# The first rows of a decoder trunk, each transfer split by partitions over two issuing engines

## The chip, the cores and the metric

The kernel runs on one NeuronCore of one Trainium2 chip. The engines are named as the profile names them: PE (TensorE; PEld is its weight load), ACT (ScalarE), DVE (VectorE), POOL (GpSimd) and SP (SyncE, which issues transfers and computes nothing). The metric is the device time of one execution in microseconds (us), as the median of several runs. A profile is one more execution, taken with the hardware profiler; it has a time of its own, and a span from the first to the last instruction.

## The reference

The reference is a two-layer decoder trunk over 256 tokens of width 1024, all in float32. Layer 0 has a gated short convolution as its mixer, layer 1 an attention over shared keys and values. Each layer has a half-step feed-forward block before and after its mixer. The change touches only the start of the first block, which computes this:

```
def rmsnorm(x, g):
    y = x * lax.rsqrt(jnp.mean(x * x, axis=-1, keepdims=True) + EPS)
    return y * g

def swiglu_ffn(x, w_in, w_out):
    gate, up = jnp.split(x @ w_in, 2, axis=-1)
    return (jax.nn.silu(gate) * up) @ w_out

h = h + 0.5 * swiglu_ffn(rmsnorm(h, ffn1_norm[0]), ffn1_w_in[0], ffn1_w_out[0])
```

D_MODEL is 1024, D_FF 2816. Everything after it (mixers, attention, the other three feed-forward blocks) is the same in both kernels.

## The kernel before

**Layout.** The activations stay in SBUF, transposed: `h[c]` for c from 0 to 7 holds 128 features (partitions) by 256 tokens. A matmul is done in split precision: every operand is a high part (rounded to the fp32r type) and a low part (the rest). The high weights meet high and low activations in one matmul of 512 columns, the low weights meet the high activations in a second one of 256 columns. So every weight is first cast by ACT to its high part (`wh`) and subtracted by DVE for its low part (`wl`), and every activation likewise: ACT writes the high half of `xs` (line 293), DVE the low half (line 297).

**Weight stream.** All weights come from HBM through a class `Stream`: 1 MB pieces into one of three staging buffers `ws`, issued by SP at line 131, then cast by line 166 and subtracted by line 189. SP holds back a piece until its staging buffer is free.

**The first rows.** To start PE early, the first weight tiles (`f` 0 and 1, gate and up) do not go through the stream. On the host they are laid out between the rows of the input: the array `first` has, for each of the 128 partitions, 84 columns of gains and convolution taps, and then for every feature tile k a block of 768 columns, 256 of `x` and 512 of weights. It lands in the tile `base`. The list `cut` (line 242) divides it into seven column ranges, each a transfer over all 128 partitions, issued by SP in a loop (lines 243 and 244):

| transfer | columns | bytes in a row | KB | what it completes |
|---|---|---|---|---|
| 1 | gains, k = 0: x and weights of f = 0 | 2384 | 298 | group (0) for f = 0 |
| 2 | k = 0: weights of f = 1 | 1024 | 128 | group (0) |
| 3 | k = 1 | 3072 | 384 | group (1) |
| 4 | k = 2 | 3072 | 384 | group (2) |
| 5 | k = 3 | 3072 | 384 | group (3) |
| 6 | k = 4, 5 | 6144 | 768 | group (4,5) |
| 7 | k = 6, 7 | 6144 | 768 | group (6,7) |

After them SP issues the first two halves of a weight piece (line 252) and two more pieces (line 131).

**ACT at the start.** Its first instruction, line 247, is an activation on a single column that makes ACT load its function table while nothing else is to be done. Then it waits for the first transfer.

**PE at the start.** Eight fp32 matmuls on a tile of ones (line 257, two passes each in the trace) run while the first transfer is under way. Their results are not used.

**The work on the first rows** is `first_tiles` (lines 486 to 520). For every group of `GROUPS` it goes: high and low parts of `xs` (ACT line 293, DVE line 297), high and low parts of the weights for both f (ACT line 496, DVE line 497), after groups (1) and (3) the squares of two tiles for the norm (ACT line 484), and then PE's matmuls, high weights at line 505 and low weights at line 508, eight in all for a group of one tile. The sum of squares and its square root come later, in `first_rms`, because the scale can be applied after the matmul.

**What sets the order.** The kernel is scheduled by hand: each engine runs its instructions in the order of the program text. The framework adds the semaphores. A transfer counts a completion semaphore up as it lands; instructions that read the data wait for it. An instruction that waits holds back all that stands behind it on its engine; that holds for transfers which an engine issues, too.

Of the kernel before, what the change touches and what calls it, by code (L numbers as in the profile page):

```python
# [16 lines left out]
P = 128  # L17
# [43 lines left out]
def trunk(ctx, tc, A, out):  # L61
    nc = tc.nc
    ve, ac, pe, po, sy = nc.vector, nc.scalar, nc.tensor, nc.gpsimd, nc.sync
# [13 lines left out]
    def one(shape, name, dt=F32):  # L77
        return cp.tile(list(shape), dt, tag=name, name=name)
# [159 lines left out]
    base = one([P, G_N + ND * KW], "base")  # L238
# [2 lines left out]
    h = [kt8[:, c, :T] for c in range(ND)]  # L241
    cut = [G_N + KW - 2 * P, G_N + KW] + [G_N + (g[-1] + 1) * KW for g in GROUPS[1:]]
    for lo, hi in zip([0] + cut, cut):
        sy.dma_start(base[:, lo:hi], A["first"][:, lo:hi])
    epst = one([P, 1], "epst")
    po.memset(epst, EPS)
    ac.activation(mk([P, 1], "warm", 1), epst, AF.Sqrt)
# [1024 lines left out]
```

## Time and profile before

| | us |
|---|---|
| median of 3 runs | 975.01 (974.86 to 975.71) |
| the profiled execution | 975.94 |
| its span, first to last instruction | 974.0 |
| PE busy | 967.4 (99%) |
| DVE busy | 735.3 (75%) |
| ACT busy | 560.6 (58%) |
| POOL busy | 163.7 (17%) |

The profile page gives busy times of the engines, and a chain of work that ended last, followed back from the last instruction. Its other views are used below: the order in time of a stretch (each row a start, a duration, an engine, a source line, what is written and read, and in brackets the idle time of the engine before it and what ended it), who waited for whom, groups of instructions by line, and busy times by window. Lines are those of the kernel text above. The trace's clock starts with the span. The two microseconds between the span and the execution's time lie outside what the profile shows.

The granted clock of PE is 1.000 as a mean over the span.

### The profile page before, as it was taken

How to read it: one execution, taken by the hardware profiler on the slowest of the kernel's cores; microseconds unless marked ns; L12 is line 12 of the kernel's file. 1: busy time of each engine (PE TensorE's matmuls, PEld its weight loads, DVE VectorE, ACT ScalarE, POOL GpSimd, SP SyncE). 2: the span in 40 equal slices, each digit the busy share in tenths (PEclk: the TensorE clock that was granted, in tenths of full speed). 3: DMA queues.
4: the chain of work that ended last, by engine and by line, in shares of the span. 5: the costliest groups of instructions: out<-in, count | busy, mean ns of one | idle time of the engine just before them, and what ended most of it. 6: DMA issues, size and time to landing. Idle time of an engine off the chain costs nothing.

```text
span 974.0 us, 14801 instructions
## 1 busy us (share of the span) xinstructions
PE 967.4 (99%) x5728; PEld 848.3 (87%) x5728; DVE 735.3 (75%) x1167; ACT 560.6 (58%) x940; POOL 163.7 (17%) x256
## 2 busy tenths in 40 slices
PE   8999999999999999999999999999999999999998
PEld 7888888888888888888888888888987888888888
DVE  6988776668889887767649987965688888877752
ACT  7666553355556665644556667644488666656530
POOL 0000001144470100011211013001257240000000
PEclk9999999999999999999999999999999999999999
DMA  8665564546546875555535566554520445555550
GB/s 303 217 196 193 179 211 173 183 169 210 184 139 226 261 240 174 191 199 184 205 130 174 180 223 208 210 182 176 212 88 2 135 168 193 196 179 201 189 189 22
DMA packets 28290, 177.61 MB, mean 182 GB/s; under 512 B 3083, under 2 KB 6539, under 8 KB 7612
## 3 DMA queue, kind: packets, MB, share of 16 engines
q1 hardware_dynamic: 28220, 176.66, 53.4%
q8 instruction: 45, 0.74, 0.3%
q14 instruction: 25, 0.20, 0.1%
HBM read 175.57 MB, written 1.08 MB: 181 GB/s over the span
## 4 chain that ended last, share of the span: by engine, by line
PE 98%; DMA 1%; DVE 0%; SPq 0%; ACT 0%; issue 0%; DVEq 0%
PE mm L346 36%; PE mm L349 19%; PE a L455 17%; PE a L457 9%; PE a L346 3%; PE a L349 1%; PE mm L1012 1%; PE a L645 1%; PE a L647 1%; PE a L646 1%; DMA base<-in_first_dram 1%; PE a L1077 1%; PE a L1057 1%; PE a L933 1%; PE mm L528 1%; PE a L935 1%
## 5 line engine op out<-in xcount | busy, mean ns | idle before, releaser
L189 DVE TENSOR_TENSOR wl<-ws,wh 128x1024 fp32r<-128x1024 f32 x317 | 390.2, 1246 | 93.2 <-PE a L457 63.6
L346 PE MATMUL mm<-xs,wh 128*128 128x512 f32 x1480 | 355.8, 391 | 0.0
L166 ACT CAST wh<-ws 128x1024 fp32r<-128x1024 f32 x317 | 327.6, 1046 | 39.4 <-PE a L455 21.8
L346 PEld LDWEIGHTS mm<-xs,wh 128*128 128x128 f32 x1480 | 271.4, 188 | 52.2
L349 PEld LDWEIGHTS mm<-xs,wl 128*128 128x128 f32 x1480 | 191.0, 191 | 8.0
L349 PE MATMUL mm<-xs,wl 128*128 128x256 f32 x1480 | 193.6, 283 | 0.0
L455 PE MATMUL a<-act,wh 128*128 128x512 f32 x722 | 171.1, 390 | 0.0
L455 PEld LDWEIGHTS a<-act,wh 128*128 128x128 f32 x722 | 133.3, 188 | 26.4
L359 DVE TENSOR_TENSOR t<-mm,t 128x512 f32<-128x512 f32 x96 | 66.0, 688 | 68.7 <-ACT t L358 68.1
L358 ACT COPY t<-mm 128x512 f32<-128x512 f32 x96 | 56.1, 585 | 89.8 <-PE mm L349 88.2
L457 PEld LDWEIGHTS a<-act,wl 128*128 128x128 f32 x722 | 91.7, 191 | 2.8
L457 PE MATMUL a<-act,wl 128*128 128x256 f32 x722 | 92.9, 283 | 0.0
L293 ACT ACTIVATE xs<-base 128x256 fp32r<-128x256 f32 x48 | 24.1, 507 | 91.8 <-DVE base L422 77.6
L375 ACT ACTIVATE t<-t 128x256 f32<-128x256 f32 x88 | 36.8, 419 | 64.7 <-DVE t L363 64.7
L363 DVE TENSOR_TENSOR t<-t,R 128x512 f32<-128x512 f32 x88 | 61.6, 700 | 2.6
L352 ACT CAST act<-t 128x256 fp32r<-128x256 f32 x96 | 39.0, 407 | 29.1 <-DVE t L576 18.3
L311 POOL TENSOR_TENSOR t<-base 128x256 f32<-128x256 f32 x35 | 26.3, 751 | 135.4 <-DVE base L422 109.6
L353 DVE TENSOR_TENSOR act<-t,act 128x256 fp32r<-128x256 f32 x96 | 40.9, 426 | 5.7 <-ACT act L352 5.7
L308 POOL TENSOR_TENSOR sq<-base 128x256 f32<-128x256 f32 x5 | 3.1, 615 | 246.9 <-DVE base L422 235.4
L297 DVE SCALAR_TENSOR_TENSOR xs<-base,xs 128x256 fp32r<-128x256 f32 x48 | 29.1, 610 | 18.4 <-ACT xs L293 18.4
L376 DVE TENSOR_TENSOR t<-t,t 128x256 f32<-128x256 f32 x88 | 36.9, 420 | 4.3 <-ACT t L375 4.3
L422 DVE SCALAR_TENSOR_TENSOR base<-a,base 128x256 f32<-128x256 f32 x78 | 32.8, 421 | 7.7 <-PE a L457 6.3
(253 smaller groups left out, 866.3 us busy)
## 6 DMA issues: line engine op xcount, KB each, us to landing
ws<-in_ffn_w_in_dram SPq DMA_DIRECT2D x85, 1024.0 KB, 4.9
ws<-in_ffn_w_out_dram SPq DMA_DIRECT2D x44, 1024.0 KB, 4.8
ws<-in_conv_w_in_dram SPq DMA_DIRECT2D x12, 1024.0 KB, 4.8
ws<-in_w_kv_dram SPq DMA_DIRECT2D x6, 1024.0 KB, 4.8
ws<-in_conv_w_out_dram SPq DMA_DIRECT2D x4, 1024.0 KB, 4.8
ws<-in_attn_w_q_dram SPq DMA_DIRECT2D x4, 1024.0 KB, 4.9
ws<-in_attn_w_o_dram SPq DMA_DIRECT2D x4, 1024.0 KB, 4.9
base<-row_d SPq DMA_DIRECT2D x8, 256.0 KB, 6.4
```

The lines of the kernel that those rows point to most:

```text
L166: ac.copy(h, src)
L189: ve.tensor_tensor(out=l, in0=src, in1=h.bitcast(F32), op=ALU.subtract)
L346: pe.matmul(o, u[0][:, k * P:(k + 1) * P], xs[k], start=(k == 0), stop=False)
L349: pe.matmul(o[:, :T], u[1][:, k * P:(k + 1) * P], xs[k][:, :T], start=False, stop=(k == last))
L352: ac.copy(dst[:, :T], src)
L353: ve.tensor_tensor(out=dst[:, T:], in0=src, in1=dst[:, :T].bitcast(F32), op=ALU.subtract)
L358: ac.copy(r, o[:, :, T:])
L359: ve.tensor_tensor(out=r, in0=o[:, :, :T], in1=r, op=ALU.add)
L363: ve.tensor_tensor(out=r, in0=r, in1=R[:, None, :].to_broadcast([P, n, T]), op=ALU.mult)
L376: ve.tensor_tensor(out=s, in0=s, in1=r[:, 1], op=ALU.mult)
L455: pe.matmul(o, run[k][0], lhs[k], start=(k == 0), stop=False)
L457: pe.matmul(o[:, :T], run[k][1], lhs[k][:, :T], start=False, stop=(k == n - 1))
```

## The change

The loop body that issues one transfer of 128 partitions becomes a loop over two issuing engines. SP (`sy`) issues partitions 0 to 63 of the range, ACT (`ac`) partitions 64 to 127. The loop runs in the same place and over the same seven ranges. In ACT's order the seven new issues stand ahead of line 247.

```diff
     cut = [G_N + KW - 2 * P, G_N + KW] + [G_N + (g[-1] + 1) * KW for g in GROUPS[1:]]
     for lo, hi in zip([0] + cut, cut):
-        sy.dma_start(base[:, lo:hi], A["first"][:, lo:hi])
+        for eng, rows in ((sy, slice(0, P // 2)), (ac, slice(P // 2, P))):
+            eng.dma_start(base[rows, lo:hi], A["first"][rows, lo:hi])
```

The bytes, the rows and their lengths are the same; there are fourteen transfers in place of seven.

## Prediction

> **What bounds the kernel now.** I read the chain of work that ended last first, then the order in time of the first 14 us, because every line of the change is spent before 4 us. The page says of the whole span:
>
> ```profile
> span 974.0 us, 14801 instructions
> ...
> PE 98%; DMA 1%; DVE 0%; SPq 0%; ACT 0%; issue 0%; DVEq 0%
> ```
>
> TensorE (PE) carries the chain nearly from end to end; the change can only matter through the 1% that is DMA. The chain of the first 40 us shows where that is (start us, us, what):
>
> ```profile
> 3.06 8.45 DMA base<-in_first_dram
> 11.51 0.02 issue
> 11.54 0.91 ACT xs L293 x2
> 12.45 0.52 ACT wh L496
> ...
> 13.01 1.20 PE mm L505 x4
> ```
>
> The sixth first transfer lands at 11.51, ScalarE (ACT) prepares it, and from 13.01 on PE runs with hardly a hole. So the end of the program moves by what the matmul of 13.01 moves by, plus any slower matmuls behind it. The order in time before that point (start us, us, engine, line, idle before it in brackets):
>
> ```profile
> 0.73 1.28 ACT L247 ACT_TABLE_LOAD   x1 [0.73 <-PEq L1261]
> 0.74 3.23 SPq L244 DMA_DIRECT2D base<-in_first_dram  x7
> 1.05 3.45 PE L257 MATMUL a<-ones 128*128 128x128 f32 x16 [1.05 <-DVE ones L237]
> 2.03 0.20 ACT L247 ACTIVATE warm<-epst 128x1 f32<-128x1 f32 x1
> 3.84 0.51 ACT L293 ACTIVATE xs<-base 128x256 fp32r<-128x256 f32 x1 [1.61 <-DMA base<-in_first_dram]
> 4.01 1.92 SPq L252 DMA_DIRECT2D ws<-in_ffn_w_in_dram  x2
> 5.01 0.70 PE L505 MATMUL mm<-xs,wh 128*128 128x512 f32 x2 [0.51 <-ACT wh L496]
> 5.97 1.49 SPq L131 DMA_DIRECT2D ws<-in_ffn_w_in_dram  x2
> 6.08 0.51 ACT L293 ACTIVATE xs<-base 128x256 fp32r<-128x256 f32 x1 [1.13 <-DMA base<-in_first_dram]
> 7.25 0.70 PE L505 MATMUL mm<-xs,wh 128*128 128x512 f32 x2 [0.61 <-ACT wh L496]
> 8.70 0.51 ACT L293 ACTIVATE xs<-base 128x256 fp32r<-128x256 f32 x1 [0.88 <-DMA base<-in_first_dram]
> 9.71 0.51 ACT L293 ACTIVATE xs<-base 128x256 fp32r<-128x256 f32 x1
> 9.87 0.70 PE L505 MATMUL mm<-xs,wh 128*128 128x512 f32 x2 [0.98 <-ACT wh L496]
> 10.41 0.40 PE L508 MATMUL mm<-xs,wl 128*128 128x256 f32 x2
> 10.73 0.72 ACT L484 ACTIVATE t<-base 128x256 f32<-128x256 f32 x2
> 11.81 0.40 PE L508 MATMUL mm<-xs,wl 128*128 128x256 f32 x2
> ```
>
> Two things are to be seen. ACT waits for a landing three times, 1.61, 1.13 and 0.88 us, so it has slack early. But from 8.70 it runs through to 11.45 (10.73 + 0.72), 0.09 before its next start: whatever pushes ACT by more than that slack pushes PE. PE itself has holes of 0.61 and 0.98 us that lateness would fill first.
>
> **What a split transfer costs.** Seven issues on SyncE (SP) become fourteen, seven on SP and seven on ACT. The price of one issue by its rows (min/median/max ns), for 128 rows and for the 32 rows of a small table:
>
> ```profile
> L244 SPq DMA_DIRECT2D base<-in_first_dram x7: 388/432/432, 0.7 to 3.5; - x7
> ...
> L271 SPq DMA_DIRECT2D rb<-in_rel_bias_dram x1: 341/341/341, 263.9 to 263.9; - x1
> ```
>
> A quarter of the rows costs 341 ns against 432, so I take an issue to be a fixed cost: halving the rows saves at most 0.1 us each. SP's seven stay at 3.23 us in all (0.47 with the gap); nothing is won there. The bytes, their order and their engines' work stay too: 2 x 64 rows of the same length. The stream is already at the engines' limit before the waiting begins:
>
> ```profile
> 3.00:4.00 1.00, 1.00 (x7) 1.00 (x7) 0.00 (x0) 0.16 (x1) 0.10 (x1) 1.00 0.95 262
> ...
> 12.00:13.00 1.00, 0.91 (x6) 0.62 (x5) 0.90 (x3) 1.00 (x4) 0.00 (x0) 1.00 1.04 401
> ```
>
> The last two columns are the DMA engines' busy share and GB/s: busy 0.95 with 262 GB/s where rows are short, 401 where they are 6 KB. I keep the landings where they are: 3.84, 6.08, 8.70, 11.51. No row shows two queues feeding at once; a better overlap could bring the stream towards 401 GB/s, a worse one or unequal shares could delay it; I keep 0.8 us either way for the landing of the third transfer. [...]
>
> **What is new is on ACT.** Its seven issues stand ahead of the table load and of everything that ACT prepares, and behind them PE waits. No row shows ACT issuing; the nearest are SP's, from 0.34 us up to 0.96 (two of L252 in 1.92, the longest of the trace's start). I take 0.47 with the gap, the row of these very transfers; the ends are worth -0.1 and +0.5 where it counts, at the last issue. At this pace seven would take 0.74 + 3.23 = 4.0, and the table load and the warm activation of L247 (1.28 and 0.20) would end at 5.5. That alone costs nothing: the first rival.
>
> But an issue also has to wait. SP's waits in the first 20 us (total, times, longest):
>
> ```profile
> SPq L131 <- DMA ws<-in_ffn_w_in_dram: 7.2, 1, 7.2
> SPq L131 <- DMA base<-in_first_dram: 1.2, 1, 1.2
> ```
>
> The transfers that SP issues are seven of L244, two of L252, two of L131 (until 5.97 + 1.49 = 7.46), and the next, the twelfth, first waits 1.2 us for a *first* transfer, until 8.7. It does not read those rows; what lands at 8.7 is the fourth first transfer (ACT's start at 8.70 waits for it). Twelve minus four is eight: a transfer takes over the completion counter of the one eight places before it and waits until that has landed. I assume that both queues draw from one rotation, in program order; the trace, with one queue, cannot show it.
>
> With fourteen halves numbered SP 1, ACT 1, SP 2, ACT 2 and so on, halves 1 to 4 of each queue are free, and halves 5, 6 and 7 wait for halves 1, 2 and 3 of the same queue. ACT then goes: four issues, 0.74 to 2.6; the fifth waits for the first landing, 3.84, issue to 4.3; the sixth follows, to 4.8 (2 landed by then); the seventh waits for the third pair, 6.08, and is issued at 6.51; table load to 7.8, warm to 8.0, and the first xs of L293 starts at about 8.05 instead of 3.84: 4.2 us later. The rows that would cover a late ACT are the waits of 1.13 and 0.88 us; 4.2 is more than their sum.
>
> From there ACT has no wait left. Group 2 and 3 took 11.45 - 8.70 = 2.75 (2.66 up to where the next activation could overlap), groups 0 and 1 the same kind of work, so 5.3 in all: the xs of group (4,5) starts at 13.4 instead of 11.54, **+1.85**. PE's side: first matmul at 5.01 + 4.2 = 9.2, four groups at 1.40 (10.41 to 11.81), next at 14.85 instead of 13.01, **+1.85** as well. SP's later loads do not matter: each waits for a half eight places ahead, the fourth and fifth pairs first, and these land before 11.51, while the engines still have the sixth and seventh to move.
>
> **The clock.** PE's warm-up ends at 1.05 + 3.45 = 4.50; the next matmul now comes at 9.2, a hole of 4.7 us instead of 0.51. What a hole does is seen at both ends of the trace: the warm-up's matmuls before 3.7 and after 4.1, and the windows after the last matmul (970.9), where the column before the last two is the granted clock:
>
> ```profile
> L257 PE MATMUL a<-ones 128*128 128x128 f32 x12 | 2.9, 434 | 1.1 <-DVE ones L237 1.1
> ...
> L257 PE MATMUL a<-ones 128*128 128x128 f32 x4 | 0.7, 309 | 0.0
> ...
> 970.90:973.30 2.40, 0.00 (x0) 0.00 (x0) 0.42 (x1) 0.00 (x0) 0.00 (x0) 1.00 0.16 55
> 973.40:974.00 0.60, 0.00 (x0) 0.00 (x0) 0.00 (x0) 0.00 (x0) 0.00 (x0) 0.50 0.00 0
> ```
>
> After 2.4 to 2.5 us without a matmul the clock is halved, and at the start some 3 us of matmuls (1.05 to about 4) were needed until they ran at full speed. So a hole of 4.7 probably halves the clock, and 1 to 5 us of matmuls then run at half speed: a loss of 0.5 to 2.5, of which I take 1.4. The lower end, nothing, stays in the range. [...]
>
> **Sum.** Against the profiled execution (975.94 us, of it 974.0 span): +1.85 for ACT's late start, +1.4 for the clock, 0 for SP and the bytes: +3.2. The median of the runs is 975.01, 0.93 below that execution, so I forecast **978.2 us**. A hidden 0.1 us from added semaphore waits on ACT is within the bounds.
>
> **Rivals.**
> - *ACT is not held* (20%): the second queue has counters of its own, or waits that never bite. ACT's first xs is at 5.5; groups 0 and 1 take until 5.5 + 2.7 = 8.2, still ahead of the landing of 8.70. Late start swallowed, time 975.0, give or take 0.4. It decides at one point: whether ACT's seventh issue comes before or after 6 us. Against it: SP's wait of 1.2; for it: no trace of a second queue.
> - *Held, but the clock stays* (20%): +1.85, so 976.9, between 976.1 if the third pair lands 0.8 earlier and 977.7 if later. For it: a hole of 4.7 is not much over what was seen; the switch can fall badly or well.
> - *Two queues feed better* (4%): the landing of 11.51 comes up to 1.5 us earlier since 262 GB/s become 400, and ACT is not held; PE's holes of 0.61 and 0.98 go: 973.5. Against it: engines busy at 0.95 already, and ACT's 0.09 us of slack before 11.54.
> - *Issues of both queues exclude each other*: then eight issues end at 4.4 instead of 2.6 and ACT's seventh at about 7.2: +0.65 on the forecast, 978.9; it is inside the forecast's range.
>
> **How the numbers follow.** Forecast (held, clock halved) 56%, own range 976.9 to 980.5: 975.01 + 1.85 + 0.5 - 0.5 at the low end, with 2.5 for the clock and 0.8 for a later third landing, +0.3 for waits, at the high end. The other three cases reach down to 973.5; 974.7 to 980.5 leaves out the 4%, the lowest part of the first rival and what lies above 980.5. A measurement here tells about 0.2%, 1.95 us, from no change. Slower by more: nearly all of the forecast, 0.55, and 0.4 of the held-without-clock case, 0.08: 0.63. Faster by more would need 973.06 or less: 0.03. The rest, 0.34, is the same.
>
> **What would show it.** In the changed trace, by step: ACT's DMA issues last until after 6 us, the seventh starting as the third pair lands; the table load of L247 starts near 6.5 and the first xs of L293 near 8; PE's hole before L505 is some 4.7 us; PE's matmuls of L505 after it are longer than 0.4 us, and the granted clock shows 0.5 in a stretch between 7 and 14; the matmul that stood at 13.01 stands near 16. Wrong it would be if the table load starts before 5 (ACT not held), if the first landing or the third moves by over 1 us (two queues do change the stream), or if after the late start the clock stays at 1.0.

## The result, and the profile after

The changed kernel is slower. Six runs of each, on one chip, gave 980.12 us (979.76 to 982.09) with the change and 975.62 (974.86 to 976.12) without; the ratio of the times is 1.0052, with a 95% interval of 1.0039 to 1.0065. The profiled execution took 979.88 us against 975.94 before. Two of the six runs, 981.67 and 982.09, had a mean granted clock of 0.997 and 0.999; the other four lie between 979.76 and 980.31.

The page of the changed kernel says of the whole span (3.9 us longer) and of the chain that ended last:

```profile
span 977.9 us, 14817 instructions
...
PE 98%; DMA 0%; DVE 0%; ACT 0%; ACTq 0%; issue 0%; DVEq 0%
```

PE still carries nearly the whole chain, so the loss has to be looked for where the chain starts. The chain of the first 40 us (start us, us, what):

```profile
1.95 4.72 DMA base<-in_first_dram
...
6.70 0.47 ACTq L245
...
7.20 1.28 ACT L248
...
8.61 0.49 ACT xs L294
9.10 0.61 ACT wh L497 x2
...
9.76 1.19 PE mm L506 x2
```

Before, this chain went from the sixth landing through `xs` to a matmul at 13.01. Now it goes through ACT's own issues: a half of the third transfer lands at 6.67 (1.95 + 4.72), only then, at 6.70, does ACT make its seventh issue, and behind it come the function table, `xs`, `wh` and PE's first real matmul. The order in time of the same stretch (start us, us, engine, line, idle before it in brackets; lines are one further down than before):

```profile
0.73 6.44 ACTq L245 DMA_DIRECT2D base<-in_first_dram  x7
0.74 6.71 SPq L245 DMA_DIRECT2D base<-in_first_dram  x7
...
7.20 1.28 ACT L248 ACT_TABLE_LOAD   x1 [7.20 <-DMA base<-in_first_dram]
...
9.76 1.19 PE L506 MATMUL mm<-xs,wh 128*128 128x512 f32 x2 [4.92 <-ACT wh L497]
...
16.41 0.91 ACT L294 ACTIVATE xs<-base 128x256 fp32r<-128x256 f32 x2 [0.60 <-DMA base<-in_first_dram]
...
16.78 1.08 PE L506 MATMUL mm<-xs,wh 128*128 128x512 f32 x4
```

The table load starts at 7.20 instead of 0.73, the first real matmul at 9.76 instead of 5.01, and the matmul of group (4,5) at 16.78 instead of 13.01: 3.77 us later, nearly the 3.9 by which the span grew. Line 528, the first matmul on the weights behind `first`, moved by 3.66 (18.88 to 22.54).

SyncE waited too. Its waits in the first 30 us (total, times, longest) show three at the issues of these transfers themselves, which need no data that lands:

```profile
SPq L245 <- DMA base<-in_first_dram: 2.5, 3, 1.3
```

PE's matmuls between 9.7 and 12.4, and then between 12.8 and 16.7, by groups (count, busy us and mean ns of one, idle before):

```profile
L506 PE MATMUL mm<-xs,wh 128*128 128x512 f32 x4 | 2.2, 663 | 4.9 <-ACT wh L497 4.9
L509 PE MATMUL mm<-xs,wl 128*128 128x256 f32 x4 | 1.3, 415 | 0.0
...
L506 PE MATMUL mm<-xs,wh 128*128 128x512 f32 x12 | 3.9, 406 | 0.0
L509 PE MATMUL mm<-xs,wl 128*128 128x256 f32 x12 | 2.4, 278 | 0.0
```

The first 2.6 us of real matmuls ran at a slow clock (663 and 415 ns against 406 and 278). The granted-clock column shows 1.00 there all the same, as it does over the slow warm-up before 3.7 us in the kernel before (434 ns a matmul there, 309 after 4.1): at the start of these two traces the durations tell the clock, not that column.

What the forecast had left alone moved as well. The windows from 6 to 14 us, first of the kernel before, then of the changed one (last two columns: busy share of the DMA engines, GB/s):

```profile
6.00:14.00 8.00, 6.30 (x32) 5.03 (x31) 5.28 (x13) 6.95 (x19) 0.00 (x0) 1.00 1.01 387
```

```profile
6.00:14.00 8.00, 4.24 (x17) 3.72 (x18) 4.44 (x12) 6.79 (x19) 0.00 (x0) 1.00 1.03 260
```

The engines are as busy as before and move a third less. And the issues themselves, min/median/max in ns:

```profile
L245 ACTq DMA_DIRECT2D base<-in_first_dram x7: 472/554/618, 0.7 to 6.7; - x7
L245 SPq DMA_DIRECT2D base<-in_first_dram x7: 465/573/827, 0.7 to 7.0; - x7
```

A transfer of 64 rows costs more to issue (554 and 573 ns, median) than one of 128 did (432). "Rows" are here the partitions of a transfer, each with one row of bytes.

### The profile page after: what moved, and what is told of

The parts are those of the page before. It is cut to its first block, busy times and chain, and to the rows that moved or that the text cites. A ratio compares the mean times of both kernels' runs of the same rounds, so it can differ in the third digit from the quotient of the medians.

```text
span 977.9 us, 14817 instructions
## 1 busy us (share of the span) xinstructions
PE 968.3 (99%) x5728; PEld 849.5 (87%) x5728; DVE 735.1 (75%) x1167; ACT 560.0 (57%) x940; POOL 165.9 (17%) x256
## 3 DMA queue, kind: packets, MB, share of 16 engines
HBM read 175.57 MB, written 1.08 MB: 181 GB/s over the span
## 4 chain that ended last, share of the span: by engine, by line
PE 98%; DMA 0%; DVE 0%; ACT 0%; ACTq 0%; issue 0%; DVEq 0%
PE mm L347 36%; PE mm L350 19%; PE a L456 17%; PE a L458 9%; PE a L347 3%; PE a L350 1%; PE mm L1013 1%; PE a L646 1%; PE a L648 1%; PE a L647 1%; PE mm L506 1%; PE a L1078 1%; PE a L1058 1%; PE a L934 1%; PE mm L529 1%; PE a L935 1%
```

## The experiments

Two theories could each explain 4 us. **The hold**: ACT's issues wait for completion counters, ACT prepares nothing meanwhile, and PE starts late and at a slow clock. **The halves**: transfers of 64 neighbouring partitions move and issue more slowly, whoever issues them. The runs take them apart. The table has them all; the fifth column is by how much the first matmul of line 528 (529 to 531 elsewhere) starts later than the 18.88 of before, the last how much longer the span of the profiled execution is than 974.0. "Before" is the kernel before on the same chip.

| run | median us | before us | ratio (95%) | line 528 later | span longer |
|---|---|---|---|---|---|
| the change | 980.12 | 975.62 | 1.0052 (1.0039 to 1.0065) | 3.66 | 3.9 |
| e1_split4 | 976.50 | 975.27 | 1.0011 (1.0002 to 1.0020) | 0.17 | 0.3 |
| e2_split5 | 977.62 | 975.27 | 1.0022 (1.0012 to 1.0031) | 1.92 | 2.0 |
| e3_split6 | 978.84 | 975.27 | 1.0037 (1.0024 to 1.0050) | 3.54 | 3.6 |
| e4_sp14 | 980.56 | 975.27 | 1.0054 (1.0041 to 1.0066) | 4.26 | 4.6 |
| e5_sp14even | 986.53 | 975.46 | 1.0117 (1.0102 to 1.0132) | 10.32 | 10.6 |
| e6_evenodd | 984.62 | 975.46 | 1.0096 (1.0082 to 1.0110) | 8.23 | 8.5 |
| e7_warm26 | 979.39 | 975.46 | 1.0040 (1.0027 to 1.0052) | 3.29 | 3.6 |
| e8_holdalone | 980.37 | 975.46 | 1.0049 (1.0037 to 1.0062) | 4.48 | 4.4 |
| e9_colsplit | 980.38 | 975.33 | 1.0054 (1.0040 to 1.0068) | 3.52 | 3.5 |
| e10_sp14col | 975.98 | 975.33 | 1.0008 (0.9999 to 1.0017) | -0.48 | -0.4 |
| e11_tablefirst | 982.64 | 975.33 | 1.0077 (1.0064 to 1.0090) | 7.62 | 7.9 |
| e12_colwarm26 | 977.84 | 975.29 | 1.0026 (1.0016 to 1.0036) | 1.38 | 1.5 |

The last two columns agree within 0.4 us in every row: what the start loses arrives at the end, and nothing behind line 528 gives it back or adds to it. The medians rise by somewhat more than the spans (the change 4.5 against 3.9, e9 5.05 against 3.5): the profiled execution of the kernel before was 0.3 to 0.7 above its own medians, and those of the change, e9 and e12 were 0.24, 0.87 and 0.41 below theirs.

### Splitting only the first transfers

Three runs split the first 4, 5 or 6 of the seven transfers and leave the rest whole, on SyncE.

```diff
-    for lo, hi in zip([0] + cut, cut):
-        for eng, rows in ((sy, slice(0, P // 2)), (ac, slice(P // 2, P))):
+    for n, (lo, hi) in enumerate(zip([0] + cut, cut)):
+        halves = ((sy, slice(0, P // 2)), (ac, slice(P // 2, P))) if n < 4 else ((sy, slice(0, P)),)
+        for eng, rows in halves:
```

(5 and 6 in place of 4 for the other two.) Expected of the first:

> Only the first four of the seven transfers are split; the last three are whole, from SP. Theory H (hold): the eight halves use eight completion counters, ACT waits for none; its four issues end near 3.2 us as in the changed kernel's trace, table load to 4.5, first xs at 4.8, first real matmul at 5.95, and the landing of 8.70 swallows it: 975.6 us, within 0.5 of the kernel before. Theory S (stream): two queues of halves are slower in themselves, the loss of 4.5 us goes with the number of split transfers: 4 of 7, about +2.6, 978.2.

of the second:

> The first five transfers are split. H: ACT's fifth issue waits for its first half (3.66 in the changed trace), ends at 4.13, table load to 5.4, first xs at 5.7, first real matmul at 6.85; groups 0 and 1 are done on ACT at 8.4, before the landing near 8.7: 975.6 to 976.3. S: 5 of 7 of 4.5, about +3.2, 978.8.

of the third:

> The first six transfers are split. H: ACT's sixth issue at 5.0 as in the changed trace, ends 5.5, table load to 6.75, first xs at 6.9, first real matmul at 8.05. ACT then ends groups 0 to 3 at 12.2 instead of 11.5: +0.65, and PE's hole of 3.2 us adds 0 to 1.5 for the clock: 976.2 to 977.8. S: 6 of 7 of 4.5, about +3.9, 979.5.

The order in time of the run with four:

```profile
0.73 2.49 ACTq L246 DMA_DIRECT2D base<-in_first_dram  x4
...
3.26 1.28 ACT L249 ACT_TABLE_LOAD   x1 [3.26 <-issue]
...
13.19 1.20 PE L507 MATMUL mm<-xs,wh 128*128 128x512 f32 x4
```

With five and with six (the table load and the first real matmul of each):

```profile
4.20 1.28 ACT L249 ACT_TABLE_LOAD   x1 [4.20 <-DMA base<-in_first_dram]
...
6.76 1.19 PE L507 MATMUL mm<-xs,wh 128*128 128x512 f32 x2 [1.92 <-ACT wh L498]
```

```profile
6.40 1.28 ACT L249 ACT_TABLE_LOAD   x1 [6.40 <-DMA base<-in_first_dram]
...
8.96 1.19 PE L507 MATMUL mm<-xs,wh 128*128 128x512 f32 x2 [4.12 <-ACT wh L498]
```

Four issues wait for nothing (the table load is released by "issue"), the fifth and the sixth for a landing. The steps from 3.26 to 4.20 to 6.40 and 7.20 fit a rotation over eight counters shared by both engines, in which the fourth pair of halves is the last that finds them free. With four, the late start is swallowed up to 0.17 us at line 528; the median of its runs is still 1.23 us above the kernel before, of which its profile, 0.3 longer in the span, shows only a part. That is outside the 0.5 that the hold's theory allowed, and far below the 978.2 of the other. With five and six the loss is more than the hold's own expectation, and less than the other's. What was added is for the most part the clock: the first four groups took 8.27 us with five (6.76 to the first matmul of group (4,5) at 15.03) and 7.69 with six (8.96 to 16.65), where 5.65 is enough at full speed (below, under the clock). With five, PE's hole of only 1.92 us was followed by some 5 us of slow matmuls (two of line 507 took 1.05 us up to 12.0, 0.63 from 12.9 on); at full speed the four groups would have been done by 12.41 (6.76 + 5.65), before the 13.01 of the kernel before.

### The halves without the hold

All fourteen halves are issued by SyncE, so ACT has nothing to issue:

```diff
-        for eng, rows in ((sy, slice(0, P // 2)), (ac, slice(P // 2, P))):
+        for eng, rows in ((sy, slice(0, P // 2)), (sy, slice(P // 2, P))):
```

> All fourteen halves are issued by SP; ACT issues nothing. H: ACT's table load stands at 0.73 as before and nothing holds it; SP's issues stretch over 14 places with the waits of the rotation, the third pair is issued at 3.1 instead of 1.65: landings up to 0.7 us later, 975.6 to 976.6. If halving the transfers itself were the cost (any queue), the time would be near that of the changed kernel, 980.

Measured: 980.56, as slow as the change. The theory of the hold as the only cause fell with this run. Its order in time, issues and windows:

```profile
14.31 0.91 ACT L294 ACTIVATE xs<-base 128x256 fp32r<-128x256 f32 x2 [1.83 <-DMA base<-in_first_dram]
...
17.77 0.91 ACT L294 ACTIVATE xs<-base 128x256 fp32r<-128x256 f32 x2 [1.52 <-DMA base<-in_first_dram]
```

```profile
L245 SPq DMA_DIRECT2D base<-in_first_dram x14: 576/595/597, 0.7 to 9.0; - x14
```

```profile
6.00:14.00 8.00, 6.08 (x32) 4.70 (x30) 3.55 (x10) 4.51 (x13) 0.00 (x0) 1.00 1.04 239
```

ACT is free, and waits for landings instead: the sixth pair is there at 14.31 (11.51 before), the seventh at 17.77. Fourteen issues of 595 ns take until 9.6, and the stream moves 239 GB/s between 6 and 14 us with the engines fully busy. The last pair lands some 8 us after its issue, so here the moving sets the end more than the issuing does. This run has no loss to the clock: its first two matmuls of line 506 take 0.70 us, as before, not 1.19.

Is it the number of transfers or which partitions they cover? The next run keeps fourteen halves by SyncE and cuts by columns, so that each half covers all 128 partitions with rows half as long:

```diff
+        mid = (lo + hi) // 2
+        for eng, x0, x1 in ((sy, lo, mid), (sy, mid, hi)):
+            eng.dma_start(base[:, x0:x1], A["first"][:, x0:x1])
```

> The same column halves, all fourteen issued by SP; ACT issues nothing. P: neither hold nor slow stream is left, only fourteen issues of 0.43 to 0.6 us in a row and the waits of the rotation: third pair landed near 6.5, group (4,5) prepared near 11.6 to 12.3, time 975.5 to 976.5 (980.56 with halves by partitions). If fourteen issues from one queue cost it by themselves: 980.5 again.

Measured 975.98, 0.65 above the kernel before, with an interval (0.9999 to 1.0017) that still holds no change. Issues, windows and order in time:

```profile
L246 SPq DMA_DIRECT2D base<-in_first_dram x14: 387/432/590, 0.7 to 6.9; - x14
```

```profile
6.00:14.00 8.00, 6.52 (x35) 5.11 (x34) 5.97 (x14) 7.10 (x19) 0.00 (x0) 1.00 0.98 344
```

```profile
12.53 1.20 PE L507 MATMUL mm<-xs,wh 128*128 128x512 f32 x4 [0.93 <-DVE xs L299]
```

So fourteen transfers by themselves cost little or nothing. It is the halves of 64 partitions that issue slowly (595 against 432 ns) and move slowly (239 against 344 GB/s). Two more runs ask whether it matters that these 64 are neighbours: even partitions in one half, odd ones in the other, first all by SyncE, then shared as in the change.

```diff
+        for eng, rows in ((sy, slice(0, P, 2)), (sy, slice(1, P, 2))):
```

```diff
+        for eng, rows in ((sy, slice(0, P, 2)), (ac, slice(1, P, 2))):
```

> As the run with all fourteen halves on SP (980.56 us), but the halves are the even and the odd partitions instead of the upper and the lower 64. Theory P (port span): 64 neighbouring partitions are written at about 250 GB/s, and partitions spread over all 128 are not; a row of 6144 B takes 234 ns again (452 in the other run), group (4,5) is prepared near 12 instead of 14.3, and the time is 975.8 to 977. Theory N (any transfer of 64 rows moves at half the rate): 980.5 again.

> The change with even partitions on SP and odd ones on ACT. Under P the stream runs near 400 GB/s once rows are long, and only ACT's hold is left: seventh ACT issue near 6.3, table load near 6.8, first xs at 8.2, first real matmul at 9.4; with the clock's loss 978.3 to 979.8, little below the changed kernel's 980.1. If the slower stream were what the changed kernel pays, the time would come back to 976 to 977.

Both times missed, 986.53 and 984.62, for a reason beside the question. ACT's first cast waited for transfers that come much later, as the order in time of the first of the two shows (in the second it waited until 13.60):

```profile
15.41 0.71 ACT L497 CAST wh<-base 128x256 fp32r<-128x256 f32 x2 [10.87 <-DMA base<-in_first_dram]
```

It looks as if every second partition counted as the whole range of partitions and columns when the framework decides who waits for whom; the trace shows the wait, not the reason. The traces still answer the question. The issues are as slow as those of neighbours, here for even and odd halves by SyncE:

```profile
L245 SPq DMA_DIRECT2D base<-in_first_dram x14: 573/595/598, 0.7 to 9.0; - x14
```

So the price of an issue goes with the 64 partitions, neighbours or not; why 64 cost more than 128 no run shows. For the moving, take ACT's queue, which carries nothing but `first`. The rows give packets, MB, and the time of the packets as a share of 16 engines; of the shared even and odd halves between 9 and 12 us, of the change between 10 and 15, and of the only queue of the kernel before between 9 and 13:

```profile
q10 hardware_dynamic: 146, 0.71, 57.1%
```

```profile
q10 hardware_dynamic: 85, 0.41, 33.3%
```

```profile
q1 hardware_dynamic: 362, 1.63, 101.3%
```

57.1% of 16 engines for 3 us is 27.4 engine-us for 0.71 MB, 38.6 us for one MB; 33.3% of 16 for 5 us is 26.6 for 0.41 MB, 65 us. The kernel before needed 40 (101.3% of 16 for 4 us, 1.63 MB). So from two queues halves of every second partition move at the rate of whole transfers (38.6 against 40), and halves of 64 neighbours take 1.7 times as long for a byte. From SyncE alone, first even and odd halves between 11 and 15 us, then neighbours between 11 and 17:

```profile
q1 hardware_dynamic: 289, 1.31, 94.2%
```

```profile
q1 hardware_dynamic: 282, 1.30, 100.3%
```

That is 46 us for one MB (94.2% of 16 for 4 us, 1.31 MB, of which up to 0.4 can be weight pieces that follow `first` on this queue) against 74 (100.3% of 16 for 6 us, 1.30 MB): again the neighbours take 1.6 times as long, but here the even and odd halves don't quite reach the 40 of whole transfers. In both comparisons the halves have 64 partitions and rows of the same length; only which partitions go together differs.

The upper and lower halves from two queues, in flight together, did not make up for each other: 260 GB/s between 6 and 14 us, where whole transfers from one queue moved 387. That 64 neighbours take longer is measured; why, no run shows, and "port span" in the expectation above is only the author's name for a theory.

### The hold without the halves

The first of two runs leaves the transfers of the kernel before whole and holds ACT with copies that nothing uses, the first of which waits for the third transfer:

```diff
     ac.activation(mk([P, 1], "warm", 1), epst, AF.Sqrt)
+    held = one([P, T], "held", mybir.dt.bfloat16)
+    for _ in range(6):
+        ac.copy(held, h[1])
```

> The kernel before (seven whole transfers from SP) with six copies of 256 columns on ACT after its table load, the first of which waits for the third transfer: ACT is held until about 8.6, and nothing of the stream is changed. If the hold makes the loss: first real matmul near 9.7, 979.3 to 980.3 with the clock's loss. If the stream of halves makes it: 975 to 976.5.

The second shares halves by columns between SyncE and ACT: the change with full-width transfers.

```diff
+        mid = (lo + hi) // 2
+        for eng, x0, x1 in ((sy, lo, mid), (ac, mid, hi)):
+            eng.dma_start(base[:, x0:x1], A["first"][:, x0:x1])
```

> The change with each transfer halved by columns instead of partitions: both halves have all 128 partitions and rows of half the length; SP issues the left half, ACT the right, the same fourteen issues. Theory P (64 neighbouring partitions are slow): rows of 3072 B take some 121 ns, the stream of the long transfers runs at 330 to 400 GB/s instead of 250, the seventh pair lands near 13.5 to 14.5 instead of 16.3. Theory H (ACT's hold sets the changed kernel's end, the stream hides behind it): first xs still at 8.2 to 8.6, time 979 to 980.3. If the stream is what the changed kernel pays: 976 to 977.5.

Measured: 980.37 and 980.38, each just over the upper end of what was expected. The order in time of the first, then of the second:

```profile
6.57 2.58 ACT L250 CAST held<-base 128x256 bf16<-128x256 f32 x6 [4.34 <-DMA base<-in_first_dram]
...
10.23 1.19 PE L508 MATMUL mm<-xs,wh 128*128 128x512 f32 x2 [5.39 <-ACT wh L499]
```

```profile
6.64 1.28 ACT L249 ACT_TABLE_LOAD   x1 [6.64 <-DMA base<-in_first_dram]
...
9.20 1.19 PE L507 MATMUL mm<-xs,wh 128*128 128x512 f32 x2 [4.37 <-ACT wh L498]
```

The hold by itself makes a loss of this size too, though the copies held ACT a little longer than the change does: PE's first real matmul comes at 10.23, in the change at 9.76. The second run also gives the forecast's numbers nearly to the digit: table load at 6.64 (forecast 6.5), first matmul at 9.20 (9.2). With full-width transfers the hold is as long as I worked out; the 0.56 us more in the change (7.20, 9.76) come from the halves.

### The clock

More matmuls on ones, 26 in place of 8 (two passes each), bridge PE's hole; first in the change, then with halves by columns.

```diff
-NWARM = 8
+NWARM = 26
```

> The changed kernel with 26 warm-up matmuls instead of 8, so that PE is busy until about 8.5 us. If the clock takes 1.4 us of the loss: PE at full speed from its first real matmul near 9.8, time 978.4, range 977.9 to 979, and no executions near 982. If the clock costs nothing: 980.1.

> The column halves on SP and ACT (980.38) with 26 warm-up matmuls instead of 8. In the changed kernel these brought group (4,5) 1.4 us forward, and 1.1 of it was lost again to the late landing of the seventh pair. Column halves land earlier: if that reading is right, nothing is given back, the first matmul after the first tiles (line 528 of the kernel before) starts near 20.9 instead of 22.4, and the time is 978.6 to 979.2. If the give-back had another reason: 979.6 to 980.2.

Measured: 979.39, 0.4 above the range expected if the clock takes 1.4 us, and 977.84, below what was expected. The first order in time is that of the change with a longer warm-up, the second that of the halves by columns with it:

```profile
9.69 0.70 PE L506 MATMUL mm<-xs,wh 128*128 128x512 f32 x2 [0.16 <-ACT wh L497]
...
15.34 1.12 PE L506 MATMUL mm<-xs,wh 128*128 128x512 f32 x4
...
16.79 0.91 ACT L294 ACTIVATE xs<-base 128x256 fp32r<-128x256 f32 x2 [1.04 <-DMA base<-in_first_dram]
...
22.17 2.11 PE L529 MATMUL mm<-xs,wh 128*128 128x512 f32 x8 [0.85 <-DVE t L360]
```

```profile
8.84 0.70 PE L507 MATMUL mm<-xs,wh 128*128 128x512 f32 x2 [0.35 <-ACT wh L498]
...
20.26 2.11 PE L530 MATMUL mm<-xs,wh 128*128 128x512 f32 x8
```

The first four groups now take 15.34 - 9.69 = 5.65 us instead of 16.78 - 9.76 = 7.02: the clock cost the change 1.37. In the change most of it is given back: line 529 is only 0.37 earlier (22.54 to 22.17), because ACT waits 1.04 for the seventh pair and PE then 0.85. With full-width halves that pair is there in time and the whole gain stays: 22.40 to 20.26, 2.14, and 2.54 in the medians. That is 0.8 us below the lower end of what I expected: the four groups took 7.42 us in the run without the longer warm-up (9.20 to 16.62) and 5.66 with it (8.84 to 14.50), so 1.76 went to the clock there, and 0.36 came from a hold that ended earlier in this execution (table load at 6.28 instead of 6.64). What remains against the kernel before, 1.38 at line 528 and 2.55 in the medians, is the hold with the clock taken care of; the change with the same warm-up keeps 3.29 and 3.93, so with the clock out of the way the halves show as a cost beside the hold.

### The table load ahead of the issues

The lines of `epst` and `warm` move above the loop, so that ACT loads its table first:

```diff
+    epst = one([P, 1], "epst")
+    po.memset(epst, EPS)
+    ac.activation(mk([P, 1], "warm", 1), epst, AF.Sqrt)
     for lo, hi in zip([0] + cut, cut):
         for eng, rows in ((sy, slice(0, P // 2)), (ac, slice(P // 2, P))):
             eng.dma_start(base[rows, lo:hi], A["first"][rows, lo:hi])
-    epst = one([P, 1], "epst")
-    po.memset(epst, EPS)
-    ac.activation(mk([P, 1], "warm", 1), epst, AF.Sqrt)
```

> The changed kernel with ACT's table load and warm activation moved ahead of its seven issues. If ACT issues transfers while its table load runs: ACT's seventh issue again near 6.7, first xs at 7.2, 1.4 earlier, and the next to be late is the stream: group (6,7) waits for the landing near 16.3, its first matmul at 17.8 instead of 15.92: +1.9 to 2.4, 977.3 to 977.9. If hold alone counts and the stream costs nothing: 976.6 to 977.2 with the clock. If the table load stops ACT's issuing until 2.0: all landings 1.3 later, 980 or more.

Measured 982.64, a miss by 5 us. The order in time:

```profile
0.73 1.28 ACT L245 ACT_TABLE_LOAD   x1 [0.73 <-PEq L1262]
0.87 1.36 ACTq L248 DMA_DIRECT2D base<-in_first_dram  x2
2.26 6.25 ACTq L248 DMA_DIRECT2D base<-in_first_dram  x5
...
17.62 0.91 ACT L294 ACTIVATE xs<-base 128x256 fp32r<-128x256 f32 x2 [1.66 <-DMA base<-in_first_dram]
```

The load does not keep ACT from issuing (0.87 lies inside it), but its last issue still ended at 8.51, later than in the change (7.17), and `xs` started at 8.55 all the same. SyncE's seven ended earlier, at 6.35 (7.45 in the change), as if the counters had been dealt in another order. Behind that the last pairs came late, and ACT waited 1.92 us for one and 1.66 for another. PE stood idle for 2.06 us over the second wait, and the first four matmuls behind it took 1.65 us instead of 1.08. The time is one that the expectation gave to a table load that stops the issues, but that is not what happened. The saved table load of 1.3 us was eaten by waits, and the run tells nothing about the hold that the others don't.

## Why the prediction was right in kind and too small

**The place and the direction** were right. ACT's seven issues stand ahead of its table load; the transfers share counters that ACT has to wait for; ACT is held, PE starts late and at a slow clock. The rival in which ACT is not held would show a table load before 5 us; it starts at 7.20. The run with four splits shows where it turns: with four issues ACT is free, and 0.17 us are left of the loss at line 528.

**The counters.** The prediction had ACT's seventh issue wait for the third pair, by counting SyncE's twelfth transfer back by eight. The chain shows it: landing at 6.67, issue at 6.70. That both queues draw from one rotation was assumed; the series of four, five, six and seven splits fits it, and the run with the table load first, where ACT's issues ended later than in the change (8.51 against 7.17) and SyncE's earlier (6.35 against 7.45), suggests that the order of the rotation isn't simply the program's.

**The step that failed** is the one on the transfers: "The bytes, their order and their engines' work stay too: 2 x 64 rows of the same length", and from it "I keep the landings where they are: 3.84, 6.08, 8.70, 11.51". The bytes stayed, the engines' work did not: 65 us of engine time for one MB in place of 40. The third pair landed at 6.67 instead of 6.08, within the 0.8 that I had left open, and the last ones later still: ACT waited for the seventh until 16.41. With it fell "halving the rows saves at most 0.1 us each": halving the rows to 64 added 0.12 to 0.16 us to an issue (554 and 573 ns in the change, 595 with SyncE alone, neighbours or not, against 432). "SP's seven stay at 3.23 us in all" fell too: they took 6.71, waits for the counters among them. The row of 32 rows with 341 ns, from which I had taken a fixed cost, was of another tensor with other rows; it did not carry that far.

**The term that was mis-sized** is the hold: +1.85 at group (4,5) was forecast. Measured there are 3.77, less 1.37 for the clock: 2.4. The difference of 0.55 is that by which the table load was late (7.20 against 6.5, partly the issue itself) and the first matmul with it (9.76 against 9.2). The run with full-width halves, where the first matmul comes at 9.20, puts it on the halves: with four groups at full speed behind it, 9.20 + 5.66 = 14.86, it gives the forecast's +1.85 again. (In the forecast's own second working, 9.2 and four groups at 1.40 make 14.8, not 14.85; nothing hangs on it.)

**The clock** was forecast at 1.4 and cost 1.37. That they agree so well is luck: the 1.4 was picked from an estimated range of 0.5 to 2.5, and the same loss was 1.76 with halves by columns. And how it came about was not as described: "a hole of 4.7 probably halves the clock" supposes a clock that was up. In the changed kernel's profile all 16 warm-up matmuls were slow, as their group says (count, busy us, mean ns):

```profile
L258 PE MATMUL a<-ones 128*128 128x128 f32 x16 | 3.8, 431 | 1.1 <-DVE ones L237 1.1
```

So in this execution the hole did not halve the clock: the slow clock of the start was still there behind it. That the hole kept it from rising is my reading; the longer warm-up in the change, which has no hole and rises (427 ns a matmul between 1 and 6 us, 279 between 6.2 and 9.6), fits it. The run with shared even and odd halves had a warm-up that did speed up (mean 400 ns), and there the granted-clock column (the third from the end) shows a halved clock in the hole, as the window from 10 to 12 us has it:

```profile
10.00:12.00 2.00, 0.00 (x0) 0.00 (x0) 0.00 (x0) 0.00 (x0) 0.00 (x0) 0.50 1.01 418
```

Both ways end with slow matmuls behind the hole: two of line 506 took 1.05 us at 11.18 in the change and at 15.51 in that run, and 0.63 once the clock was up. The granted clock of 0.5 that I named as a sign does not appear in the change's profile; by that column even my sign of being wrong, a clock that stays at 1.0, is met, and only the durations show the slow clock. The two runs with a mean of 0.997 and 0.999 may have gone the other way, which no trace here shows.

**The sum.** Against the profiled execution I had +3.25 and got +3.94 (979.88 - 975.94), 0.7 short, of which 0.55 is the hold. The rest of the miss, 980.12 against 978.2, is the base. I took 0.93 off because the profile of the kernel before lay so far above its three runs; with six runs its median was 975.62, only 0.3 below the profile, and the changed kernel's profile lay 0.24 below its own median, since two of its six runs took 2 us longer than the others.

**What the change would have cost without the hold** the prediction gave as nothing (its first rival, 975.0). The run with all halves on SyncE comes nearest to that case (its fourteen issues last until 9.6, the change's seven on each engine until 7.45), and it took 980.56. So that rival's time missed by 5.6 us: transfers of 64 neighbouring partitions lost some 5 us here with the hold (4.5) or without it (5.3).

| | full-width transfers | halves of 64 neighbours |
|---|---|---|
| ACT issues nothing | +0.65 (halves by columns, SyncE) | +5.3 (SyncE) |
| ACT issues half | +5.05 (halves by columns) | +4.5 (the change) |

Each number is a median less that of the kernel before. The two costs do not add up: while ACT is held until 8.6 us, the slow stream delivers what ACT then works off, and from there on PE has hardly a hole. That is why both together or either alone give 4.5 to 5.3, and why taking away one of them wins nothing. That the three are so near each other is partly chance: the two with the hold contain 1.4 and 1.8 us for the clock, the one without it none. No version was faster than the kernel before; the nearest, halves by columns on SyncE, can't be told from it.

What stays open is why ACT's issues ended later and SyncE's earlier with the table load first, and how much of the later landing of the third pair comes from slower issues and how much from slower transfers.

## What to carry to other kernels

Before a transfer is given to an engine that also computes, count its transfers against the completion counters: from the first issue that has to wait (here ACT's fifth), all that the engine prepares waits with it, and TensorE behind that ran at a slow clock here, which cost 1.37 us in the change. Two halves of 64 neighbouring partitions are not the same work as one whole transfer: here they moved more slowly (260 against 387 GB/s) and cost more to issue (554 and 573 against 432 ns). Where one must be split, split it by columns: from SyncE that came out 0.65 us above the kernel before, halves of neighbours 5.3. And where two costs cover each other, as the hold and the slow stream do here, taking away one shows nothing: each has to be run alone.

## What the runs showed of the hardware

- Between 6 and 14 us halves of 64 neighbouring partitions ran at 239 GB/s from one queue and 260 from two, with the DMA engines fully busy (shares 1.04 and 1.03); whole transfers ran at 387, halves by columns from one queue at 344.
- Issuing a transfer of 64 partitions took 0.60 us on SyncE, whether they were neighbours or every second one; issuing 128, with rows whole or half as long, took 0.43.
- From two queues even and odd halves needed 38.6 us of engine time for one MB, halves of neighbours 65, whole transfers from one queue 40.
- A transfer that ACT issues can start inside its table load (0.87 in a load from 0.73 to 2.01).
- The same 16 warm-up matmuls took 3.4 to 3.5 us in four of the profiles (mean 399 to 411 ns, the clock rising on the way: 434 before 3.7 us and 309 after 4.1 in the kernel before) and 3.8 in eight (431 ns, slow to the end), in kernels that do not differ until then on PE. With 52 in the warm-up of the change those between 1 and 6 us took 427 ns in the mean, those between 6.2 and 9.6 us 279; with halves by columns the 52 took 7.43 us in all, in the change 8.48. On what it depends whether and when the clock rises no run shows.
